# Projecting q, k and the third gate branch with seven products instead of eight in a two-layer encoder kernel

## The chip, the core and the metric

The kernel runs on one core of a Trainium2 chip. The metric is the device time of one execution in microseconds. Before the change it is 1118.29 us, the median of three runs (1117.27 to 1118.49). One execution was recorded with the hardware profiler; it took 1117.58 us, and its span from first to last instruction is 1115.3 us.

The engines are named as the profile names them: PE does matmuls (PEld is its weight load), DVE and ACT work elementwise, POOL does very little here, SP issues the DMAs. Each works through its own queue in order.

## The reference, cut to what matters

Two layers, each with a SwiGLU feed-forward block (FFN), a token-mixing block (mix) and a second FFN, on 256 tokens of width 1024 in float32. The change touches the mix:

```python
h = rms_norm(x, mix_pre_g[l])
u_pool, q_da, k_da, v_da, q_ca = jnp.split(h @ w_in[l], IN_SPLITS, axis=-1)
...
q = apply_partial_rope(q_da..., cos, sin)
k = apply_partial_rope(k_da..., cos, sin)
...
g_pool, g_da, g_ca = jnp.split(jax.nn.sigmoid(h @ w_gate[l] + b_gate[l]), N_BRANCH, axis=-1)
merged = (g_pool * (y_pool @ w_br_pool[l])
          + g_da * (y_da @ w_br_da[l])
          + g_ca * (y_ca @ w_br_ca[l]))
x = x + rms_norm(merged @ w_out[l], mix_post_g[l])
```

q and k together are 1024 columns of `w_in`, and so is `g_ca`, the third gate branch. Each is a product of 256x1024 tokens and a 1024x1024 weight.

## The kernel before

**Numbers in two parts.** PE multiplies fp32r, so every float32 operand is split into a high part (rounded by ACT) and a low part (the rest, by DVE), and one product is three matmuls, high x high, high x low and low x high (`mm3`, line 229, matmul at line 235). Weights come from memory in units of 128 partitions x 2048 columns (1 MB). `load_unit` (line 100) puts a unit into one of five `raw` buffers, and `split_unit` (line 113) makes its two parts in one of five pairs of tiles `wh` and `wl`: ACT casts (line 119), DVE subtracts (line 120), in two halves of 1024 columns, or in four quarters for the first five units of a stage (`fine`).

**The mix.** It has the normed, transposed tokens in an `xhl` tile (two chunks `c` of 128 tokens, eight blocks of 128 of the width). `pre_norm` (line 187) makes them while the FFN before is in its last matmuls: DVE gains and scales a chunk (lines 194 and 199), PE transposes it (line 207), ACT and DVE split it (lines 164 and 165). The mix then projects q and k (four units, 96 matmuls of 512 columns), turns them by RoPE (lines 627 to 630), transposes them for the scores (line 634), projects v (two units, 48 matmuls), then the pooling input and the cross-attention query (`form_a`, 96 matmuls of 256 columns), the memory keys and values (48), and the three gate branches (twelve units, 288). The attention's small matmuls are set between these: `place` and `issue_after` tie them to a matmul of that long row, counted in `fill`, at the positions in the `T_` tables at the top. Then `merged` (line 813) multiplies the three branches by their weights and by the gates, and `tail` (line 284) does the output projection and the norms of the next stage.

**Groups of seven in the FFNs.** The second FFN of both layers and the first of layer 1 already do some of their up-projections with Strassen's algorithm (in Winograd's form, `group`, line 384). The tokens are cut in two along the tokens and in two along the width (four blocks), the weight in four units `w11`, `w12`, `w21`, `w22`. Seven products of 12 matmuls then do the work of eight. For that, four sums of token blocks are made and split once (`token_sums`, line 374: four DVE operations of 512 columns, four ACT casts, four DVE subtracts), four sums of weight units (DVE, 128x2048, `add`, line 366), and seven sums of results (DVE, 128x512, the same line). `PLAN` sets such a group (`g`) among plain up (`u`) and down (`d`) projections. `pre_norm` keeps float32 copies of the token blocks for it (`keep`, line 212).

**Order.** The program is written in the order above; a scheduler of the framework then lays out each engine's queue by dependences and its own estimates, and buffers are taken in turn from pools of fixed depth. Weight loads go through SP's queue in the order of use.

## Time and profile before

| view | what it says |
|---|---|
| profiled execution | 1117.58 us, span 1115.3 us |
| three runs | median 1118.29 us, 1117.27 to 1118.49 |
| busy, share of the span | PEld 82%, ACT 58%, POOL 2% (PE and DVE in the prediction) |
| granted TensorE clock | 0.999 |
| weight loads | 189 of 1 MB, 4.8 us from issue to landing (median) |

How to read it: a matmul's own duration in the profile (393 ns) is longer than the distance to the next one, since matmuls are pipelined; the pieces of the chain of work show the distance. The chain of work that ended last is followed back from the last instruction, and names at each step the engine that was waited for. A row of the timeline merges instructions that follow one another: start in us, length in us, engine, line, operation, out<-in, count, and in brackets the idle time before it and what ended it.

### The profile page before, as it was taken

The page shows a single profiled execution, that of the slowest core. Times are in us where ns is not written, and L with a number is a line of the kernel's source. Part 1 is how long each engine was busy: PE and PEld are TensorE (multiplying, and loading weights), DVE is VectorE, ACT ScalarE, POOL GpSimd, SP SyncE. Part 2 cuts the span into 40 slices and gives each one's busy share as a digit, 9 for nine tenths or more (in the row PEclk, how much of TensorE's full clock was granted, in tenths as well). Part 3 has the DMA queues.
Part 4 walks back from the last instruction along what each step waited for, and adds up shares of the span by engine and source line. Part 5 has one row for each costly group of instructions (what it writes and reads, how often), then busy time and mean ns, then how long its engine had stood idle before and what let it go on. Part 6 is the DMA issues. An engine that isn't in the chain of part 4 may idle for free.

```text
span 1115.3 us, 13906 instructions
## 1 busy us (share of the span) xinstructions
PE 1106.0 (99%) x5247; PEld 912.4 (82%) x5247; DVE 892.5 (80%) x1215; ACT 652.0 (58%) x1082; POOL 25.0 (2%) x37
## 2 busy tenths in 40 slices
PE   9999999999999999999999999999999999999997
PEld 6888888888888888888888888888888888888886
DVE  6765556757857899999989999996676678999994
ACT  7656345646575557474675574765566647575571
POOL 0000000000000100000000000010000001000000
PEclk9999999999999999999999999999999999999999
DMA  9966543564563453563951736575445644273731
GB/s 343 385 239 227 214 150 130 189 227 144 198 218 139 173 205 132 209 244 135 332 199 71 302 118 221 201 269 196 170 172 191 236 158 175 89 254 138 286 114 38
DMA packets 35489, 218.27 MB, mean 196 GB/s; under 512 B 4192, under 2 KB 4448, under 8 KB 11232
## 3 DMA queue, kind: packets, MB, share of 16 engines
q1 hardware_dynamic: 35424, 217.40, 53.6%
q8 instruction: 41, 0.67, 0.2%
q14 instruction: 24, 0.20, 0.0%
HBM read 216.33 MB, written 1.05 MB: 195 GB/s over the span
## 4 chain that ended last, share of the span: by engine, by line
PE 97%; DMA 1%; ACT 1%; DVE 0%; POOL 0%; issue 0%; SPq 0%; DVEq 0%; POOLq 0%; ACTq 0%
PE ma L235 52%; PE acc L277 26%; PE mb L235 9%; PE acc L235 5%; PE mb L325 2%; PE mb L207 1%; PE acc L672 1%; PE acc L695 1%; PE mb L564 1%; DMA hid<-in_xt 1%; PE acc L758 1%; DMA raw<-in_w 0%; PE acc L742 0%; PE mb L831 0%; PE mb L634 0%; ACT wh L119 0%
## 5 line engine op out<-in xcount | busy, mean ns | idle before, releaser
L120 DVE TENSOR_TENSOR wl<-raw,wh 128x1024 fp32r<-128x1024 f32 (+1 forms) x498 | 524.5, 1093 | 99.2 <-ACT wh L119 96.8
L119 ACT CAST wh<-raw 128x1024 fp32r<-128x1024 f32 (+1 forms) x498 | 445.0, 949 | 198.0 <-DVE raw L366 62.1
L235 PE MATMUL ma<-wh,xhl 128*128 128x512 f32 x1664 | 529.8, 393 | 0.7 <-ACT wh L119 0.7
L235 PEld LDWEIGHTS ma<-wh,xhl 128*128 128x128 f32 x1664 | 311.5, 188 | 66.3 <-ACT wh L119 1.8
L235 PE MATMUL ma<-wl,xhl 128*128 128x512 f32 x832 | 327.0, 393 | 0.2 <-DVE wl L120 0.2
L277 PE MATMUL acc<-wh,hid 128*128 128x512 f32 x704 | 228.1, 395 | 0.0
L235 PEld LDWEIGHTS ma<-wl,xhl 128*128 128x128 f32 x832 | 156.4, 188 | 32.7 <-issue 1.0
L277 PEld LDWEIGHTS acc<-wh,hid 128*128 128x128 f32 x704 | 132.2, 188 | 27.0
L277 PE MATMUL acc<-wl,hid 128*128 128x512 f32 x352 | 136.7, 390 | 0.0
L235 PE MATMUL mb<-wh,xhl 128*128 128x512 f32 x280 | 90.4, 389 | 0.0
L366 DVE TENSOR_TENSOR raw<-raw 128x2048 f32<-128x2048 f32 x36 | 82.4, 2288 | 0.4
L277 PEld LDWEIGHTS acc<-wl,hid 128*128 128x128 f32 x352 | 66.3, 188 | 12.6
L235 PEld LDWEIGHTS mb<-wh,xhl 128*128 128x128 f32 x280 | 52.6, 188 | 10.9
L235 PE MATMUL mb<-wl,xhl 128*128 128x512 f32 x140 | 54.5, 389 | 0.0
L235 PE MATMUL acc<-wh,xhl 128*128 128x512 f32 x160 | 51.6, 391 | 0.0
L340 ACT ACTIVATE s<-ma 128x256 f32<-128x256 f32 x24 | 8.9, 386 | 64.6 <-PE ma L235 64.3
L148 POOL TENSOR_TENSOR sm<-sm,mhalf 128x1 f32<-128x1 f32 (+1 forms) x26 | 22.0, 846 | 1002.0 <-DVE sm L157 822.8
L155 ACT ACTIVATE junk<-acc 128x512 bf16<-128x512 f32 x24 | 14.4, 599 | 48.0 <-PE acc L277 48.0
L277 PE MATMUL acc<-wh,xhl 128*128 128x512 f32 x128 | 40.7, 394 | 0.0
L164 ACT CAST hid<-mb 128x256 fp32r<-128x256 f32 x88 | 32.1, 370 | 13.1 <-PE mb L325 10.3
L165 DVE TENSOR_TENSOR hid<-mb,hid 128x256 fp32r<-128x256 f32 x88 | 36.6, 419 | 1.6 <-ACT hid L164 1.4
L235 PEld LDWEIGHTS acc<-wh,xhl 128*128 128x128 f32 x160 | 30.0, 188 | 6.1
(161 smaller groups left out, 882.7 us busy)
## 6 DMA issues: line engine op xcount, KB each, us to landing
raw<-in_w SPq DMA_DIRECT2D x189, 1024.0 KB, 4.8
gain<-in_gains SPq DMA_DIRECT2D x17, 512.0 KB, 4.2
raw<-in_w SPq DMA_DIRECT2D x8, 256.0 KB, 5.6
hid<-in_memt SPq DMA_DIRECT2D x8, 256.0 KB, 7.5
hid<-in_xt SPq DMA_DIRECT2D x4, 256.0 KB, 5.3
raw<-in_w SPq DMA_DIRECT2D x2, 512.0 KB, 7.3
x<-in_x SPq DMA_DIRECT2D x4, 256.0 KB, 6.6
hid<-in_mem SPq DMA_DIRECT2D x4, 256.0 KB, 7.5
```

What stands on the lines that cost most here:

```text
L119: high = nc.scalar.copy(out=h[:, cs], in_=raw[:, cs])
L120: low = nc.vector.tensor_tensor(out=l[:, cs], in0=raw[:, cs], in1=h.bitcast(F32)[:, cs], op=ALU.subtract)
L148: nc.gpsimd.tensor_tensor(out=r, in0=v, in1=mhalf[:, :n], op=ALU.pow)
L155: sq.append(nc.scalar.activation(out=junk, in_=h, func=AF.Square, scale=fold / 32.0, accum_out=s[:, i:i + 1]))
L164: high = nc.scalar.copy(out=h, in_=ps)
L165: return high, nc.vector.tensor_tensor(out=l, in0=ps, in1=h.bitcast(F32), op=ALU.subtract)
L207: tps.append(nc.tensor.transpose(out=ps[:, k * P:(k + 1) * P], in_=xn[:, i * P:(i + 1) * P], identity=ident))
L235: done.append(nc.tensor.matmul(out=out, lhsT=lhsT, rhs=rhs, start=(first and i == 0), stop=(last and i == n - 1)))
L277: done.append(nc.tensor.matmul(out=banks[b], lhsT=a, rhs=ww[:, k, fs], start=(kk == first and k == 0 and i == 0), stop=(kk == last and k = ...
L325: nc.tensor.transpose(out=tp[:, u * P:(u + 1) * P], in_=hn[:, u * P:(u + 1) * P], identity=ident)
L366: nc.vector.tensor_tensor(out=out, in0=a, in1=b, op=ALU.add)
L564: ins.append(nc.tensor.transpose(out=tp[:, i * P:(i + 1) * P], in_=a[:, hh, kt * P:(kt + 1) * P], identity=ident))
```

## The change

q and k become one Strassen group at the start of the mix, with the first chunk of v in front of it and the second chunk of v in its middle. The first two gate branches stay as they are; the third becomes a second group at the end of the gates. Both use the same four token sums, which `token_sums` now makes once in the mix and which stay in one pair of `wh` and `wl` tiles until the second group is done. So of the five `wl` tiles, three are left for weights after the first group: `kv` (v and other results) keeps one as before, the sums another; of the five `wh` tiles `qkT` keeps one as before and the sums another. `pre_norm` now keeps the float32 token blocks for the mix too. The two `xhl` buffers become two named tiles, `xa` and `xb`, chosen by `slot`. The tokens of the memory (`mem_gain`) are no longer asked for in the FFN before, but in the mix, behind q and k. The results of the second half of q, k come out with a minus sign, which the copy of kT turns around (`sign`), as the bias addition does for the gates. The signs apart, what is computed is the same.

Core of the diff (`tokens_of`, `product`, `add`, `sums_tile` and `token_sums` are the FFN's helpers, moved out and made general; `...` marks what is left out):

```diff
-T_ROPE = 13
+T_ROPE = (13, 40)
...
-T_KT = (200, 222)
+T_KT = (152, 174)
...
-    xts = ctx.enter_context(tc.tile_pool(name="xts", bufs=2))
+    xts = ctx.enter_context(tc.tile_pool(name="xts", bufs=1))
...
+    def product(out, at, w):
+        wv = [t.rearrange("p (k m) -> p k m", k=4) for t in w]
+        return mm3(out, [(at(k), (wv[0][:, k, :], wv[1][:, k, :])) for k in range(4)])
+
+    def tokens_of(xx, c, b):
+        return lambda k: (xx[0][:, c, 4 * b + k, :], xx[1][:, c, 4 * b + k, :])
+
+    def add(out, a, b):
+        nc.vector.tensor_tensor(out=out, in0=a, in1=b, op=ALU.add)
+
+    def sums_tile(slot):
+        if slot is None:
+            sums = [wts.tile([P, 4 * 4, P], F32R, name=n) for n in ("wh", "wl")]
+        else:
+            t = xts.tile([P, 2, 4 * 4, P], F32R, name=("xa", "xb")[slot])
+            sums = [t[:, 0], t[:, 1]]
+        return sums, lambda j: (lambda k: (sums[0][:, 4 * j + k, :], sums[1][:, 4 * j + k, :]))
+
+    def token_sums(kept, sums):
+        a11, a12, a21, a22 = (kept[c, b] for c in range(2) for b in range(2))
+        s1 = t2()
+        nc.vector.tensor_tensor(out=s1, in0=a22, in1=a21, op=ALU.subtract)
+        nc.vector.tensor_tensor(out=a21, in0=a11, in1=a21, op=ALU.subtract)
+        nc.vector.scalar_tensor_tensor(out=a11, in0=s1, scalar=-1.0, in1=a11, op0=ALU.mult, op1=ALU.subtract)
+        nc.vector.scalar_tensor_tensor(out=a12, in0=a11, scalar=-1.0, in1=a12, op0=ALU.mult, op1=ALU.subtract)
+        for j, t in enumerate((s1, a11, a21, a12)):
+            split(t.rearrange("p (k t) -> p k t", t=P), sums[0][:, 4 * j:4 * j + 4, :], sums[1][:, 4 * j:4 * j + 4, :])
...
+        sums, summed = sums_tile(None)
+
+        def v_half(c):
+            ps = ma_bank()
+            now = form_b2(ps, ws[0], ws[1], c, xx)
+            nc.scalar.copy(out=v[:, c, :], in_=ps)
+            return now
+
+        qk = [s4.tile([P, D], F32, name="s4") for _ in range(2)]
+        s, u2, u3, v1 = (qk[c][:, b * 512:(b + 1) * 512] for c in range(2) for b in range(2))
+        ws = [next_unit() for _ in range(2)]
+        done = v_half(0)
+        w11, w12, w22, w21 = (next_raw() for _ in range(4))
+        pa, pe = ma_bank(), ma_bank()
+        done += product(pa, tokens_of(xx, 0, 0), split_unit(w11, 2))
+        nc.scalar.copy(out=u2, in_=pa)
+        done += product(pe, tokens_of(xx, 0, 1), split_unit(w21, 2))
+        add(s, u2, pe)
+        issue_after(late, done[T_UP])
+        token_sums(kept, sums)
+        v_half(1)
+        add(w11, w11, w12)
+        pd = mb_bank()
+        product(pd, summed(0), split_unit(w11, 2))
+        add(w11, w11, w22)
+        add(w12, w12, w22)
+        pb = mb_bank()
+        product(pb, summed(1), split_unit(w11, 2))
+        add(u2, u2, pb)
+        add(w21, w21, w11)
+        pc = ma_bank()
+        product(pc, summed(2), split_unit(w12, 2))
+        add(u3, u2, pc)
+        add(u2, u2, pd)
+        add(v1, u3, pd)
+        pf = mb_bank()
+        product(pf, summed(3), split_unit(w22, 2))
+        add(u2, u2, pf)
+        pg = ma_bank()
+        product(pg, tokens_of(xx, 1, 1), split_unit(w21, 2))
+
+        qkT = wts.tile([P, 2, 2, HEADS, P], F32, name="wh")
...
-        ws = [next_unit() for _ in range(4)]
-        done, wait = [], []
+        placed, fill = [], []
+        w = next_unit()
+
+        def place(at):
+            placed.append((at, []))
+            return placed[-1][1]
+
...
         for c in range(2):
-            qk = s4.tile([P, D], F32, name="s4")
-            for p in range(2):
-                ps = ma_bank()
-                now = form_b2(ps, ws[2 * p], ws[2 * p + 1], c, xx)
-                done += now
-                if c == 0 and p == 1:
-                    issue_after(late, done[T_UP])
-                issue_after(wait, now[T_ROPE])
-                wait = []
-                nc.scalar.copy(out=qk[:, p * 512:(p + 1) * 512], in_=ps)
-            g = qk.rearrange("p (g d) -> p g d", d=64)
+            if c == 1:
+                add(u3, u3, pg)
+            g = qk[c].rearrange("p (g d) -> p g d", d=64)
...
-            for dst, off in ((qT, 0), (kT, 512)):
+            wait = place(T_ROPE[c])
+            for dst, off, sign in ((qT, 0, 1.0), (kT, 512, -1.0)):
                 tp = mb_bank()
...
-                nc.scalar.copy(out=dst[:, c], in_=tp.rearrange("p (h t) -> p h t", h=HEADS))
-
-        mm = mm()
-        ws = [next_unit() for _ in range(2)]
-        fill, placed = [], []
-
-        def place(at):
-            placed.append((at, []))
-            return placed[-1][1]
-
-        for c in range(2):
-            ps = ma_bank()
-            now = form_b2(ps, ws[0], ws[1], c, xx)
-            fill += now
-            issue_after(wait, now[T_ROPE])
-            wait = []
-            nc.scalar.copy(out=v[:, c, :], in_=ps)
-
-        w = next_unit()
+                    wait.append(nc.tensor.transpose(out=tp[:, h * P:(h + 1) * P], in_=qk[c][:, off + h * P:off + (h + 1) * P], identity=ident))
+                nc.scalar.activation(out=dst[:, c], in_=tp.rearrange("p (h t) -> p h t", h=HEADS), func=AF.Copy, scale=sign)
+        mm = mem_gain(l, 1 - slot)
+
...
-        for br in range(3):
+        for br in range(2):
...
+        bias = gain(l * 10 + 9)
+        s, u2, u3, v1 = (hids.tile([P, 512], F32, name="hid") for _ in range(4))
+        w11, w12, w22, w21 = (next_raw() for _ in range(4))
+
+        def gate_product(at, w):
+            ps = ma_bank()
+            fill.extend(product(ps, at, split_unit(w, 2)))
+            return ps
+
+        nc.scalar.copy(out=s, in_=gate_product(tokens_of(xx, 0, 0), w11))
+        add(w11, w11, w12)
+        nc.scalar.copy(out=v1, in_=gate_product(summed(0), w11))
+        add(w11, w11, w22)
+        add(w12, w12, w22)
+        add(u2, s, gate_product(summed(1), w11))
+        add(u3, u2, gate_product(summed(2), w12))
+        add(u2, u2, v1)
+        add(v1, u3, v1)
+        add(s, s, gate_product(tokens_of(xx, 0, 1), w21))
+        add(w21, w21, w11)
+        add(u2, u2, gate_product(summed(3), w22))
+        add(u3, u3, gate_product(tokens_of(xx, 1, 1), w21))
+        for (b, c), t, sign in (((0, 0), s, 1.0), ((1, 0), u2, -1.0), ((0, 1), u3, 1.0), ((1, 1), v1, -1.0)):
+            nc.vector.scalar_tensor_tensor(out=t, in0=t, scalar=sign, in1=bias[:, b * 512:(b + 1) * 512], op0=ALU.mult, op1=ALU.add)
+            gates[2, b, c] = t
...
-                nx["xx"] = xt_pair()
-                nx["kept"] = {} if stages[i + 1][0] == "ffn" else None
+                nx["slot"] = slot if kind == "ffn" else 1 - slot
+                nx["xx"] = xt_pair(nx["slot"])
...
         wi = a["w_in"][l]
-        for s in (256, 768, 1280):
-            wide(wi, slice(s, s + 512))
+        wide(wi, slice(1280, 1792))
+        for half, col in ((0, 256), (0, 768), (1, 768), (1, 256)):
+            block(wi, half, col)
         for s in (0, 1792):
             cols(wi, slice(s, s + 256))
         wide(a["w_mem_kv"][l], slice(0, 512))
-        for i in range(6):
+        for i in range(4):
             wide(a["w_gate"][l], slice(512 * i, 512 * i + 512))
+        for half, col in ((0, 2048), (0, 2560), (1, 2560), (1, 2048)):
+            block(a["w_gate"][l], half, col)
         br = np.concatenate([a["w_br_pool"][l], a["w_br_da"][l], a["w_br_ca"][l]], axis=0)
         for i in range(2):
```

**What moves on DVE at the start of the mix.** The names: line 157 to 199 (the same in both) is the norm of chunk 1, line 165 on `xhl` or `xa` the split of its transposed tokens, line 120 a weight's low part, line 176 the memory tokens, 627 to 630 RoPE. DVE's queue of before, from the norm of chunk 1:

```order
L157 TENSOR_SCALAR sm<-sm 128x1
L194 TENSOR_TENSOR s_1652<-x_89,gain 128x512 x2
L199 TENSOR_SCALAR s_1652<-s_1652,sm 128x512 x2
L120 TENSOR_TENSOR wl<-raw,wh 128x512 x2
L176 SCALAR_TENSOR_TENSOR xhl<-hid,colt,xhl 128x2x128 x5
L165 TENSOR_TENSOR xhl<-mb,xhl 128x512 x2
L176 SCALAR_TENSOR_TENSOR xhl<-hid,colt,xhl 128x2x128 x3
L627 TENSOR_TENSOR s_1791<-s_1738,csd 128x256
L628 TENSOR_TENSOR s_1792<-s_1738,snd 128x16x8
L629 TENSOR_TENSOR s_1792<-s_1738,snd 128x16x8
L630 TENSOR_TENSOR s_1738<-s_1791,s_1792 128x16x16
```

And of the change, where line 275 is `add` and lines 288 to 291 are the sums in `token_sums`:

```order
L199 TENSOR_SCALAR s4_1647<-s4_1647,sm_1657 128x512 x2
L120 TENSOR_TENSOR wl_1751<-raw_1740,wh_1750 128x1024
L165 TENSOR_TENSOR xa_1561<-mb_1661,xa_1561 128x512
L165 TENSOR_TENSOR xa_1561<-mb_1670,xa_1561 128x512
L120 TENSOR_TENSOR wl_1751<-raw_1740,wh_1750 128x1024
L120 TENSOR_TENSOR wl_1770<-raw_1746,wh_1769 128x1024 x2
L288 TENSOR_TENSOR s2_1788<-s2_1677,s2_1668 128x512
L275 TENSOR_TENSOR raw_1740<-raw_1740,raw_1742 128x2048
L275 TENSOR_TENSOR s4_1688<-s4_1688,ma_1749 128x512
L289 TENSOR_TENSOR s2_1668<-s2_1585,s2_1668 128x512
L165 TENSOR_TENSOR wl_1687<-s2_1788,wh_1686 128x512
L290 SCALAR_TENSOR_TENSOR s2_1585<-s2_1788,s2_1585 128x512
```

(`wl_1751` is the low part of `w11`, `wl_1770` that of `w21`, `wl_1687` holds the token sums, `raw_1740` is `w11` itself.) Before, chunk 1's norm was followed by the rest of k's last unit, the memory tokens and RoPE; now it is followed by the low parts of `w11` and `w21`, and then by a row of sums. In layer 0 the memory tokens have gone ahead of the norms, into the last part of the FFN. Behind the rows shown, DVE goes on with the three other token sums and their splits, three weight sums in a row, and the low parts of the other five products, with six sums of results among them.

**What moves on PE there.** Names with their buffer numbers: `mb_1666` and `mb_1673`, now `mb_1661` and `mb_1670`, take the transposes of chunk 1's tokens. Before, from the end of k's first unit:

```order
L235 MATMUL ma_1765<-wl_1717,xhl_1570 128x512
L235 MATMUL ma_1765<-wh_1716,xhl_1570 128x512
L235 MATMUL ma_1765<-wh_1728,xhl_1570 128x512
L207 MATMUL mb_1666<-ident_92,s4_1652 128x128 x4
L207 MATMUL mb_1673<-ident_92,s4_1652 128x128 x4
L235 MATMUL ma_1765<-wl_1729,xhl_1570 128x512
L235 MATMUL ma_1765<-wh_1728,xhl_1570 128x512 x2
```

And of the change, from the end of v's first chunk (`ma_1714`), where `ma_1748` is the product with `w11` and `ma_1749` that with `w21`:

```order
L235 MATMUL ma_1714<-wl_1705,xa_1561 128x512
L235 MATMUL ma_1714<-wh_1704,xa_1561 128x512
L235 MATMUL ma_1748<-wh_1750,xa_1561 128x512
L235 MATMUL ma_1749<-wh_1769,xa_1561 128x512
L207 MATMUL mb_1661<-ident_92,s4_1647 128x128 x4
L207 MATMUL mb_1670<-ident_92,s4_1647 128x128 x4
L235 MATMUL ma_1748<-wl_1751,xa_1561 128x512
L235 MATMUL ma_1748<-wh_1750,xa_1561 128x512 x2
```

Before, 36 matmuls and one more of the mix stood ahead of the transposes. Now it is 26: the 24 of v's first chunk and one each of the products with `w11` and `w21`, those that need only a high part; the two products' other matmuls follow the transposes.

**What moves on DVE at the end of the gates.** Lines 796 (before) and 823 (change) add a gate's bias to a finished bank, line 535 and 543 look for a softmax's maximum, 747 and 774 are its reciprocal, 752 its scaling, 705 to 715 and 732 to 742 the attention's norm. Before, around the last score matmuls:

```order
L705 TENSOR_SCALAR sm_2346<-sm_2337 128x4
L708 TENSOR_TENSOR s2_2350<-acc_2286,sm_2348 128x512
L120 TENSOR_TENSOR wl_2764<-raw_2761,wh_2763 128x1024 x2
L715 SCALAR_TENSOR_TENSOR xhl_2239<-mb_2352,gsub_104,xhl_2239 128x512
L120 TENSOR_TENSOR wl_2772<-raw_2769,wh_2771 128x1024
L796 TENSOR_TENSOR hid_2687<-ma_2662,gain_2617 128x512
L535 TENSOR_REDUCE sm_2372<-acc_2359 128x2
L535 TENSOR_REDUCE sm_2372<-acc_2360 128x2
L120 TENSOR_TENSOR wl_2772<-raw_2769,wh_2771 128x1024
L537 TENSOR_SCALAR sm_2375<-sm_2372 128x4
L120 TENSOR_TENSOR wl_2834<-raw_2831,wh_2833 128x1024 x2
L747 RECIPROCAL sm_2383<-sm_2371 128x4
```

And of the change, where `raw_2805` is the second group's `w11`, `raw_2807` its `w12`, `raw_2809` its `w22`, and `ma_2772` the last plain gate:

```order
L275 TENSOR_TENSOR raw_2805<-raw_2805,raw_2807 128x2048
L275 TENSOR_TENSOR raw_2807<-raw_2807,raw_2809 128x2048
L732 TENSOR_SCALAR sm_2386<-sm_2377 128x4
L823 TENSOR_TENSOR hid_2770<-ma_2745,gain_2657 128x512
L735 TENSOR_TENSOR s2_2390<-acc_2326,sm_2388 128x512
L120 TENSOR_TENSOR wl_2836<-raw_2805,wh_2835 128x1024 x2
L742 SCALAR_TENSOR_TENSOR xb_2279<-mb_2392,gsub_104,xb_2279 128x512
L823 TENSOR_TENSOR hid_2797<-ma_2772,gain_2657 128x512
L275 TENSOR_TENSOR raw_2805<-raw_2805,raw_2809 128x2048
L543 TENSOR_REDUCE sm_2412<-acc_2399 128x2
L543 TENSOR_REDUCE sm_2412<-acc_2400 128x2
L120 TENSOR_TENSOR wl_2858<-raw_2805,wh_2857 128x1024
```

Three of the four weight sums of the second group stand here among the softmax, each 2048 columns wide, and the low parts in between belong to its products. Before, there were only low parts.

More of the change, by code (lines that the diff above doesn't have):

```diff
@@ L168, in halves, with xt_pair @@
         return [t[:, 0:512], t[:, 512:1024]]
-    def xt_pair():
-        t = xts.tile([P, 2, 2, KT, P], F32R, name="xhl")
+    def xt_pair(slot):
+        t = xts.tile([P, 2, 2, KT, P], F32R, name=("xa", "xb")[slot])
         return t[:, 0], t[:, 1], t.rearrange("p s c k t -> p (s c) k t")
@@ L295, in tail, with ffn @@
         return tps
-    def ffn(i, xx, late, kept, g_post, finish, ahead, raw_rstd=None):
+    def ffn(slot, xx, late, kept, g_post, finish, ahead, raw_rstd=None):
         fine[0] = FINE
@@ L355, in up_both @@
                 if kept and p == 2 and c == 0:
[L356 to L360 removed]
+                    token_sums(kept, sums)
         def tokens(c, b):
[L363 to L366 removed]
+            return tokens_of(xx, c, b)
         if kept:
[L369 to L382 removed]
+            sums, summed = sums_tile(1 - slot)
         def group(p):
@@ L584, in mem_gain, with mix @@
             loaded.append(t)
-        def scaled():
-            for b, t in enumerate(loaded):
-                for i in range(2):
-                    k = 2 * b + i
-                    col = 3 * DEPTH + KT + KT * l + k
-                    gained_split((mm[0][:, :, k, :], mm[1][:, :, k, :]), t[:, i], colt[:, col:col + 1])
-            return mm
-        return scaled
-    def mix(l, xx, late, mm, finish):
+        for b, t in enumerate(loaded):
+            for i in range(2):
+                k = 2 * b + i
+                col = 3 * DEPTH + KT + KT * l + k
+                gained_split((mm[0][:, :, k, :], mm[1][:, :, k, :]), t[:, i], colt[:, col:col + 1])
+        return mm
+    def mix(l, slot, xx, late, kept, finish):
         fine[0] = FINE
@@ L600, in mix @@
         colb = l * 3
-        qkT = wts.tile([P, 2, 2, HEADS, P], F32, name="wh")
-        qT, kT = qkT[:, 0], qkT[:, 1]
         kv = wts.tile([P, 2048], F32, name="wl")
@@ L606, in mix @@
         kc = kv[:, 1536:2048].rearrange("p (t s) -> p t s", t=2)
+        sums, summed = sums_tile(None)
[15 more added lines that the diff above has]
+        issue_after(late, done[T_UP])
+        token_sums(kept, sums)
+        v_half(1)
[19 more added lines that the diff above has]
+        qkT = wts.tile([P, 2, 2, HEADS, P], F32, name="wh")
+        qT, kT = qkT[:, 0], qkT[:, 1]
         held = rawp.tile([P, 2048], F32, name="raw")
@@ L806, in mix @@
         preload(AF.Silu, sg)
-        mg = xt_pair()
+        mg = xt_pair(slot)
         turns = []
@@ L882, in finish @@
             if c == 0:
-                nx["xx"] = xt_pair()
-                nx["kept"] = {} if stages[i + 1][0] == "ffn" else None
+                nx["slot"] = slot if kind == "ffn" else 1 - slot
+                nx["xx"] = xt_pair(nx["slot"])
+                nx["kept"] = {}
                 nx["g"] = gain(stages[i + 1][1] * 10 + stages[i + 1][2])
@@ L892, in ahead @@
                     mem_scale()
-                if row == 0:
-                    nx["mem"] = mem_gain(l)
-            late = ffn(i, cur, late, kept, gain(l * 10 + row + 1), finish, ahead, [rst[:, c:c + 1] for c in range(2)] if i == 0 else None)
-        else:
-            late = mix(l, cur, late, mem, finish)
-        cur, mem, kept = nx.get("xx"), nx.get("mem"), nx.get("kept")
+            late = ffn(slot, cur, late, kept, gain(l * 10 + row + 1), finish, ahead, [rst[:, c:c + 1] for c in range(2)] if i == 0 else None)
+        else:
+            late = mix(l, slot, cur, late, kept, finish)
+        slot, cur, kept = nx.get("slot"), nx.get("xx"), nx.get("kept")
 def _constants(np):
```

29 lines of the change are left out of this document (5 added, 24 removed).

## The prediction

> **What bounds the kernel now.** I read the page first, then the chain of waits, then stretches and single rows. The page's rows of busy time and of the chain:
>
> ```profile
> span 1115.3 us, 13906 instructions
> PE 1106.0 (99%) x5247; PEld 912.4 (82%) x5247; DVE 892.5 (80%) x1215; ACT 652.0 (58%) x1082; POOL 25.0 (2%) x37
> ...
> PE 97%; DMA 1%; ACT 1%; DVE 0%; POOL 0%; issue 0%; SPq 0%; DVEq 0%; POOLq 0%; ACTq 0%
> ```
>
> 97% of the chain is PE, so a matmul taken out is worth its distance to the next one, as long as nothing else comes last. The distance stands in the chain, in order of time, in a stretch of 48 matmuls; the rows below it are the start of the mix of layer 0 (the transposes of chunk 0, the first matmuls, the transposes of chunk 1) and, for later, the first product of a group of the FFN:
>
> ```profile
> 31.12 10.94 PE ma L235 x48
> ...
> 191.77 0.87 PE mb L207 x8
> 192.65 2.09 PE acc L277 x9
> 194.74 8.39 PE ma L235 x37
> 203.13 0.87 PE mb L207 x8
> ...
> 427.65 5.44 PE mb L235 x24
> ```
>
> 10.94 / 48 = 0.228 us a matmul. The pieces join: PE does not wait from 191.77 to 204.00. An average hides how near DVE is, so the next view is busy time in stretches: two in the FFN of layer 0 that already has groups of seven, then the mix's start, and from the memory's keys to the last gate.
>
> ```profile
> core 0: us, PE busy (x) PEld busy (x) DVE busy (x) ACT busy (x) POOL busy (x), PEclk, DMA share, GB/s
> 407.00:425.00 18.00, 18.00 (x87) 14.91 (x86) 17.44 (x22) 7.23 (x15) 0.00 (x0) 1.00 0.14 57
> 425.00:457.00 32.00, 32.00 (x146) 26.47 (x145) 30.96 (x34) 23.98 (x30) 0.00 (x0) 1.00 0.60 223
> ...
> 194.60:229.90 35.30, 35.30 (x170) 29.49 (x168) 25.75 (x46) 22.61 (x41) 2.08 (x2) 1.00 0.58 208
> ...
> 243.50:339.50 96.00, 95.74 (x487) 78.20 (x488) 65.95 (x112) 59.79 (x126) 2.06 (x2) 1.00 0.50 178
> ```
>
> Where a group stands, DVE is 97% busy, with PE still fed. In the mix's start it is 73% busy (25.75 of 35.30), in the gates 69%. That is the room there is.
>
> **The change, part by part.** *Matmuls.* Two groups of seven per layer instead of eight products each: 12 fewer matmuls a group, 48 in all, 48 x 0.228 = 10.9 us, 5.5 a layer. This is certain, the program has 48 fewer at line 235.
>
> *What a group costs DVE.* The rows by form, and a pair of rows of the timeline where such instructions stream:
>
> ```profile
> L120 DVE TENSOR_TENSOR wl<-raw,wh 128x1024 fp32r<-128x1024 f32 x378 | 448.7, 1221 | 88.9 <-ACT wh L119 86.7 <-issue 1.3 <-PE ma L235 0.4
> L366 DVE TENSOR_TENSOR raw<-raw 128x2048 f32<-128x2048 f32 x36 | 82.4, 2288 | 0.4
> L366 DVE TENSOR_TENSOR s<-s,mb 128x512 f32<-128x512 f32 x36 | 24.7, 687 | 0.9 <-PE mb L235 0.9
> ...
> 220.15 4.63 DVE L120 TENSOR_TENSOR wl<-raw,wh 128x1024 fp32r<-128x1024 f32 x4
> ...
> 408.50 4.61 DVE L366 TENSOR_TENSOR raw<-raw 128x2048 f32<-128x2048 f32 x2
> ...
> 417.50 0.69 DVE L165 TENSOR_TENSOR xhl<-s,xhl 128x512 fp32r<-128x512 f32 x1
> 418.10 0.69 DVE L379 SCALAR_TENSOR_TENSOR s<-s,s 128x512 f32<-128x512 f32 x1
> ```
>
> In a stream an instruction starts a little before its predecessor ends: a low half takes 1.16 us (4.63 / 4), a weight sum 2.26, an operation of 512 columns 0.60 (418.10 - 417.50). A group is 14 low halves, 4 weight sums and 7 sums of results: 16.2 + 9.0 + 4.2 = 29.4 us of DVE, against 84 x 0.228 = 19.1 us of PE. So a group starves PE unless DVE enters it some 10 us ahead.
>
> *The group of q and k.* In the changed order DVE does nothing for the group until chunk 1's norm is over. That norm waits on ACT, so its rows of before set the clock:
>
> ```profile
> 191.12 1.67 ACT L119 CAST wh<-raw 128x512 fp32r<-128x512 f32 x3 [0.61 <-PE acc L277]
> 192.70 1.06 ACT L164 CAST xhl<-mb 128x512 fp32r<-128x512 f32 x2
> ...
> 195.22 0.60 ACT L155 ACTIVATE junk<-acc 128x512 bf16<-128x512 f32 x1
> ...
> 213.69 3.93 ACT L119 CAST wh<-raw 128x1024 fp32r<-128x1024 f32 x4
> ...
> 199.35 0.21 DVE L157 TENSOR_SCALAR sm<-sm 128x1 f32<-128x1 f32 x1
> ...
> 201.21 0.88 DVE L199 TENSOR_SCALAR s<-s,sm 128x512 f32<-128x512 f32 x2 [0.44 <-POOL sm L148]
> ```
>
> From 191.12, when a `wh` tile comes free, ACT now has two half casts of w11 (0.98 each, 3.93 / 4), the pair at line 164 (1.06), a half cast of w21 and the two kept copies of chunk 0 (line 212, of the pair's size, 1.06): 196.1, where the square at line 155 stood at 195.22. So the chain behind it is 0.9 us later, and L199 ends at 203.0 instead of 202.1. From there the queue holds, in order and without a gap that I can find: 14 low halves, 4 weight sums, 4 token sums and their 4 splits, 2 splits of chunk 1 and 6 sums of results, 16.2 + 9.0 + 16 x 0.60 = 34.8 us. It is over at 237.8; the last product's second half then needs 5 more matmuls: 238.9. PE has 24 + 12 x 7 + 24 = 132 matmuls there and 0.87 of transposes, from 194.74: without a wait it would be done at 225.7. So PE waits **13.2 us**. The waits can be named: some 2 us at chunk 1's transposes, which now stand behind 26 matmuls instead of 37; about 2 for the low part of w11; 1 for w11+w12; then the largest, near 7 us with two matmuls in it, while DVE does three weight sums in a row (6.7 us) before the first low part that uses one. No later stage gives this back, since PE was not waiting before. Bounds: 12.3 if L199 keeps its old end; 15.7 with the mean durations of the rows (1221, 2288, 687 ns: 37.3 us). I take 13.2, the streamed one.
>
> *The group of the gates.* Here DVE has slack before, and two of the four weight sums stand ahead of the last plain gate. From the end of that gate's products (I call it G) DVE has 18 low halves (14 less 4 done, and the 8 of merged's four units), 2 weight sums, 8 operations of 512 columns, 4 bias additions, and the softmax, 4 maxima and 8 scalings, and 4 splits:
>
> ```profile
> L804 ACT ACT_TABLE_LOAD x2 | 2.6, 1283 | 0.0
> ...
> 298.71 1.28 DVE L535 TENSOR_REDUCE sm<-acc 128x2 f32<-128x512 f32 x2
> ...
> 304.04 1.14 DVE L752 TENSOR_SCALAR s<-s,sm 128x256 f32<-128x256 f32 x4
> ...
> 297.38 1.93 PE acc L742 x16
> 299.31 8.43 PE ma L235 x36
> 307.74 0.87 PE mb L564 x8
> ...
> 312.93 1.51 PE acc L758 x16
> ...
> 317.37 0.86 PE mb L779 x4
> ```
>
> 18 x 1.16 + 2 x 2.26 + 8 x 0.60 + 4 x 0.60 + 4 x 0.62 + 2 x 1.14 + 4 x 0.45 + 0.5 of small ones = 39.7 us. PE has to the same point 84 + 48 matmuls, 30.1 us, and 1.93 + 2 x 0.87 + 2 x 1.51 + 0.86 = 7.5 of attention: 37.6. DVE starts its list between 0.6 and 2.2 us after G, waits for ACT between 0 and 3.3 us (an estimate: ACT's own row of casts and exponentials ends about 1.6 us behind DVE's need at two places), and PE has six matmuls (1.4) behind the last low part. So PE waits between 0.6 + 39.7 + 1.4 - 37.6 = 4.1 and 2.2 + 39.7 + 3.3 + 1.4 - 37.6 = 9.0 us. ACT has twelve sigmoids in the same stretch, and three buffers are left where four were; I take 6.5, near the middle, as I could not see which of ACT's waits falls together with DVE's.
>
> *The memory tokens.* Their loads now stand behind the pool weight, which waits for a raw buffer that v's second unit frees at 180.8:
>
> ```profile
> 179.50 1.29 DVE L120 TENSOR_TENSOR wl<-raw,wh 128x512 fp32r<-128x512 f32 x2
> ...
> 185.44 0.60 ACT L155 ACTIVATE junk<-acc 128x512 bf16<-128x512 f32 x1 [3.40 <-PE acc L277]
> ...
> hid<-in_memt SPq DMA_DIRECT2D x8, 256.0 KB, 7.5
> raw<-in_poolw SPq DMA_DIRECT2D x2, 128.0 KB, 2.9
> ```
>
> In layer 0 ACT has five of their casts, and DVE five subtractions, ahead of chunk 0's squares at 185.44. With 2.9 us to land nothing is late, with 7.5 they land at 188.3 and chunk 0's transposes, which PE reaches without a wait at 191.77, are 2.9 us late. I take 1 us; layer 1 has them behind that norm, at nothing.
>
> *At nothing:* the kept copies of chunk 1 (ACT is 64% busy there, 22.61 of 35.30, and would cost 1.06 us if it were not); two more table loads a layer, since a sigmoid now stands behind the preload (1283 ns each, 2.6 us if the merge waited for ACT, which I hold inside the 9.0); the sign in the copies; RoPE, the same instructions behind the group, with the pooling's 48 matmuls to hide them; and the bytes, which stay the same.
>
> **Sum.** A layer: -5.5 + 13.2 + 6.5 = +14.2. Two layers and the 1 us: +29.4. Against the profiled execution, 1117.6, that is 1147.0; the median of the three runs is 0.7 higher: **1148**. The bounds give 1117.6 + 2 x (-5.5 + 12.3 + 4.1) = 1139 and 1117.6 + 2 x (-5.5 + 15.7 + 9.0) + 2.9 = 1159.
>
> **The rivals.** *DVE is ahead, and the matmuls count.* The price: 1118.3 - 10.9 = 1107. The place is the stretch before each group, and it decides at 10.7 us: so much of q and k's list would have to be done before L199 ends. For it: in the FFN just that happens, two weight sums begun at 408.50 are over at 413.1, and the group's products that start at 427.65 find them done 14.5 us ahead. Against it: in the mix no instruction of the list stands ahead of that norm in DVE's queue. Change by nothing, a lead of about half, is the same mechanism.
>
> *Only the first group starves.* If ACT and DVE get through the gates in time: 1118.3 + 2 x (-5.5 + 13.2) = 1134. For it: DVE is 69% busy in the gates before. Against it: the 39.7 us above against 37.6.
>
> *PE loses its rate in the waits.* The first matmuls of the program run slower than all later ones:
>
> ```profile
> 1.19 4.88 PE L869 MATMUL acc<-s 128*128 128x512 bf16 x11 [1.19 <-DVE s L866]
> ```
>
> That is 0.444 us each. If the 7 us wait brought that rate back for the four products behind it, 48 x 0.444 = 21.3 us from 226.8 would end at 248.1 instead of 238.9: 9.2 us a layer, 1166. The Trainium skill ("TensorE: Matmul & The Clock Gate", Part 1: The HAM clock gate) has a rule of this kind: PE's clock is halved after an idle window of about 3.4 us and returns after a busy one. By it the slow stretch would be short; eight matmuls of 0.444 instead of 0.228 are an estimate of 1.7 us a wait, and DVE, which sets the end of the group, would hide most of it. Nothing before the first matmuls in this trace shows such a wait, so it neither agrees nor differs. That the change does not do what it says is no rival: the 48 matmuls are gone from the program.
>
> **How the numbers follow.** Forecast (both groups starve) 0.64, only the first 0.13, the slow clock 0.08, matmuls count 0.10, within 0.2% 0.05. Faster 0.10, same 0.05, slower 0.85; 0.2%, 2.2 us, is about what a measurement of this kernel tells from no change. The range reaches from below the one-group case, 1128, to the clock's, 1168, and leaves out the 0.15 of the first and the last. The forecast's own range is 1139 to 1159.
>
> **What would show it.** The chain of waits should name DVE at lines 120 and 275 with some 13 us in q and k's stretch of each layer, and 4 to 9 in the third gate; DVE should be near 100% busy from L199 to the last low part, some 35 us; the longest gap of PE should stand before the product with w11+w22, right behind three DVE sums of 128x2048. Chunk 1's transposes should be waited for by about 2 us. It is wrong if PE stays above 97% busy through the mix's first 45 us, or if the group's weight sums stand in gaps of DVE before the norm ends.

## The result, and the profile after

| | before | change |
|---|---|---|
| median of 4 runs, us | 1117.78 | 1149.42 |
| span of the profiled run, us | 1115.3 | 1147.8 |

The ratio is 1.0284 (95% interval 1.0267 to 1.0300): 31.6 us slower, where 29.4 were forecast. From the page of the changed kernel, the rows that answer to those of before:

```profile
span 1147.8 us, 13958 instructions
...
PE 1110.5 (97%) x5199; PEld 906.3 (79%) x5199; DVE 979.2 (85%) x1299; ACT 686.3 (60%) x1124; POOL 24.9 (2%) x37
...
PE 84%; DVE 7%; ACT 4%; DMA 2%; issue 2%; POOL 1%; SPq 0%; DVEq 0%; POOLq 0%; ACTq 0%
```

PE was 97% of the chain and is 84%: 13% has passed to engines that PE waits for, DVE first. To see where, the mix is divided at three instructions that both kernels have: the transposes of chunk 0, the first score matmuls, and the first transposes of the next block. In layer 0 they stand in PE's timeline before the change as

```profile
191.61 1.03 PE L207 MATMUL mb<-ident,s 128*128 128x128 f32 x8
...
241.50 1.78 PE L672 MATMUL acc<-wh 64*128 64x256 f32 x14
...
378.65 1.04 PE L207 MATMUL mb<-ident,s 128*128 128x128 f32 x8
```

and in the changed kernel as

```profile
193.93 1.07 PE L207 MATMUL mb<-ident,s 128*128 128x128 f32 x8 [1.39 <-DVE s L199]
...
254.09 2.00 PE L699 MATMUL acc<-wh 64*128 64x256 f32 x16
...
394.88 1.04 PE L207 MATMUL mb<-ident,s 128*128 128x128 f32 x8
```

The first stretch (q, k, v and the pooling) took 49.89 us and takes 60.16, the second (gates, attention, merge, output projection) 137.15 and 140.79; 2.3 us are lost ahead of both. In layer 1 the stretches are 49.93 and 137.17 before, 61.76 and 141.63 after. 2.3 + 10.3 + 3.6 + 11.8 + 4.5 = 32.5, the difference of the spans. Each stretch also has 12 matmuls of line 235 (2.74 us) less, so PE loses 13.0 and 14.6 us in the first beside what it saves, 6.4 and 7.2 in the second. Not all of that is waiting: in the first stretch PE is idle for 8.9 and 9.3 us, where before it was not, and the rest are longer matmuls (the granted clock is 0.94 and 0.92 there, before 1.00). In the second it is idle for 4.9 and 4.5.

The 2.3 us ahead of layer 0's stretch are the memory tokens: ACT waits for their load, and the squares of chunk 0's norm (line 155) stand behind them, at 187.17 instead of 185.44:

```profile
185.96 1.31 ACT L175 ACTIVATE xb<-hid,colt 128x256 fp32r<-128x256 f32 x3 [2.03 <-DMA hid<-in_memt]
```

PE's waits in the first stretch of layer 0 (in brackets the idle time and what ended it; the last row but one is one of some ten matmuls that follow one another at a distance of 0.43 us):

```profile
207.08 0.50 PE L235 MATMUL ma<-wl,xa 128*128 128x512 f32 x1 [0.69 <-DVE wl L120]
...
219.54 0.50 PE L235 MATMUL mb<-wl,wh 128*128 128x512 f32 x1 [1.47 <-DVE wl L120]
...
225.07 0.80 PE L235 MATMUL mb<-wh 128*128 128x512 f32 x1 [4.11 <-ACT wh L119]
226.97 0.80 PE L235 MATMUL ma<-wh 128*128 128x512 f32 x1 [1.10 <-ACT wh L119]
...
228.42 0.63 PE L235 MATMUL mb<-wh 128*128 128x512 f32 x1
...
239.73 0.50 PE L235 MATMUL ma<-wl,xa 128*128 128x512 f32 x1 [0.68 <-DVE wl L120]
```

The 4.11 us are put down to ACT. ACT's row says whom it waited for, and DVE's row why:

```profile
223.97 7.68 ACT L119 CAST wh<-raw 128x1024 fp32r<-128x1024 f32 x8 [6.35 <-DVE raw L275]
```

```profile
202.68 0.88 DVE L199 TENSOR_SCALAR s<-s,sm 128x512 f32<-128x512 f32 x2
203.48 1.22 DVE L120 TENSOR_TENSOR wl<-raw,wh 128x1024 fp32r<-128x1024 f32 x1
...
219.40 6.81 DVE L275 TENSOR_TENSOR raw<-raw 128x2048 f32<-128x2048 f32 x3
226.13 4.62 DVE L120 TENSOR_TENSOR wl<-raw,wh 128x1024 fp32r<-128x1024 f32 x4
```

The cast needs the second of three weight sums in a row. From the end of the norm to 1.1 us past the group's last low part DVE is busy 35.76 of 37.30 us (engines in the order PE, PEld, DVE, ACT, POOL, then PE's clock):

```profile
203.50:240.80 37.30, 28.88 (x116) 22.03 (x115) 35.76 (x38) 17.47 (x24) 0.00 (x0) 0.91 0.29 101
```

In the second stretch most of the waiting is at the merge, past the group (all rows but the first):

```profile
329.76 0.50 PE L235 MATMUL ma<-wh 128*128 128x512 f32 x1 [0.80 <-ACT hid L834]
...
349.61 0.50 PE L235 MATMUL ma<-wh,xb 128*128 128x512 f32 x1 [0.88 <-ACT wh L119]
...
353.18 0.50 PE L235 MATMUL ma<-wl,xb 128*128 128x512 f32 x1 [1.69 <-DVE wl L120]
...
358.40 0.72 PE L235 MATMUL ma<-wh,xb 128*128 128x512 f32 x2 [0.44 <-ACT wh L119]
```

### The profile page after: what moved, and what is told of

The parts are those of the page before. It is cut to its first block, busy times and chain, and to the rows that moved or that the text cites. A ratio compares the mean times of both kernels' runs of the same rounds, so it can differ in the third digit from the quotient of the medians.

```text
span 1147.8 us, 13958 instructions
## 1 busy us (share of the span) xinstructions
PE 1110.5 (97%) x5199; PEld 906.3 (79%) x5199; DVE 979.2 (85%) x1299; ACT 686.3 (60%) x1124; POOL 24.9 (2%) x37
## 4 chain that ended last, share of the span: by engine, by line
PE 84%; DVE 7%; ACT 4%; DMA 2%; issue 2%; POOL 1%; SPq 0%; DVEq 0%; POOLq 0%; ACTq 0%
PE ma L235 42%; PE acc L305 24%; PE mb L235 9%; PE acc L235 4%; DVE wl L120 2%; DVE raw L275 2%; ACT wh L119 2%; PE mb L353 2%; DMA raw<-in_w 1%; PE acc L699 1%; PE mb L207 1%; POOL sm L148 1%; ACT junk L155 1%; DMA hid<-in_xt 1%; PE acc L785 1%
## 5 line engine op out<-in xcount | busy, mean ns | idle before, releaser
L235 PE MATMUL ma<-wh,xa 128*128 128x512 f32 x824 | 264.7, 393 | 1.5 <-ACT wh L119 1.1
L235 PE MATMUL ma<-wh,xb 128*128 128x512 f32 x680 | 219.8, 393 | 2.2 <-ACT wh L119 1.3
L235 PEld LDWEIGHTS ma<-wh,xa 128*128 128x128 f32 x824 | 154.4, 188 | 35.4 <-ACT wh L119 2.6
L235 PE MATMUL ma<-wl,xa 128*128 128x512 f32 x412 | 161.9, 393 | 3.8 <-DVE wl L120 3.8
L235 PEld LDWEIGHTS ma<-wh,xb 128*128 128x128 f32 x680 | 127.3, 188 | 29.5 <-ACT wh L119 2.1
L235 PE MATMUL ma<-wl,xb 128*128 128x512 f32 x340 | 133.6, 393 | 3.3 <-DVE wl L120 3.3
L275 DVE TENSOR_TENSOR raw<-raw 128x2048 f32<-128x2048 f32 x52 | 118.8, 2287 | 0.6
L235 PEld LDWEIGHTS ma<-wl,xa 128*128 128x128 f32 x412 | 77.4, 188 | 21.9 <-DVE wl L120 6.4
L235 PEld LDWEIGHTS ma<-wl,xb 128*128 128x128 f32 x340 | 63.9, 188 | 17.4 <-DVE wl L120 4.6
L235 PE MATMUL mb<-wh,xa 128*128 128x512 f32 x176 | 57.9, 396 | 0.0
L368 ACT ACTIVATE s<-ma 128x256 f32<-128x256 f32 x24 | 8.9, 385 | 61.3 <-PE ma L235 60.9
```

The lines of the kernel that those rows point to most:

```text
L235: done.append(nc.tensor.matmul(out=out, lhsT=lhsT, rhs=rhs, start=(first and i == 0), stop=(last and i == n - 1)))
L275: nc.vector.tensor_tensor(out=out, in0=a, in1=b, op=ALU.add)
```

## The experiments

Medians, and the two stretches of layer 0 and 1 divided as above (the ratios are to the runs of the kernel before on the same chip, whose medians lay between 1117.45 and 1117.93):

| run | median, us | ratio to before (95%) | first stretch | second stretch |
|---|---|---|---|---|
| before | 1117.8 | | 49.9, 49.9 | 137.2, 137.2 |
| change | 1149.4 | 1.0284 (1.0267 to 1.0300) | 60.2, 61.8 | 140.8, 141.6 |
| qk_only | 1142.8 | 1.0222 (1.0206 to 1.0237) | 60.4, 61.8 | 137.5, 137.6 |
| gate_only | 1131.6 | 1.0132 (1.0115 to 1.0149) | 51.7, 52.3 | 140.8, 140.9 |
| no_sums | 1126.6 | 1.0074 (1.0057 to 1.0091) | 49.9, 51.1 | 139.9, 140.8 |
| pool_sums | 1190.5 | 1.0651 (1.0636 to 1.0667) | 68.8, 70.7 | 152.0, 152.5 |
| late_preload | 1147.6 | 1.0265 (1.0251 to 1.0279) | 60.6, 60.9 | 140.0, 139.9 |
| no_sums_late | 1118.3 | 1.0007 (0.9999 to 1.0016) | 49.9, 51.2 | 135.8, 135.8 |
| memt_late | 1150.0 | 1.0286 (1.0272 to 1.0300) | 61.7, 62.0 | 140.8, 140.8 |
| warm | 1149.0 | 1.0281 (1.0267 to 1.0295) | 59.1, 61.5 | 140.8, 140.8 |
| gate_dve | 1117.9 | 1.0001 (0.9992 to 1.0010) | 49.9, 49.9 | 138.0, 138.0 |
| gate_dma | 1145.8 | 1.0255 (1.0238 to 1.0272) | 49.9, 49.9 | 151.2, 152.1 |
| both_dma | 1190.5 | 1.0649 (1.0631 to 1.0668) | 63.4, 69.2 | 154.5, 154.5 |
| shift | 1142.3 | 1.0220 (1.0206 to 1.0234) | 60.2, 61.7 | 138.0, 138.0 |

**Each group alone.** qk_only has the third gate as in the kernel before:

```diff
-        for br in range(2):
+        for br in range(3):
...
-        bias = gain(l * 10 + 9)
-        s, u2, u3, v1 = (hids.tile([P, 512], F32, name="hid") for _ in range(4))
...
```

> Only the group of q and k; the third gate stands as two plain products each, as before the change. Theory (each group is held up by DVE's own list in its own stretch): the q and k stretch is as in the change (first scores 12.6 us later than before in layer 0, of it 2.2 at the memory tokens, and 11.8 more in layer 1), and from the scores to the merge nothing is lost or won: 1117.8 + 12.6 + 11.8 = 1142 us. Rival (the loss in the gates comes from the new order, the held pair or the sigmoids, not from the group itself): the gate stretch stays 6 to 7 us a layer longer, 1155 us, since the 12 matmuls that paid for a part of it are back.

1142.8: the theory's 1142. The first stretch is the change's, the second that of before within 0.4 us. gate_only instead has q and k as plain products:

```diff
-        w11, w12, w22, w21 = (next_raw() for _ in range(4))
-        pa, pe = ma_bank(), ma_bank()
...
+        wqk = [[next_unit(), next_unit()]]
+        done += qk_half(0, 0)
...
```

> Only the group of the third gate; q and k are plain products in the order of the change, the token sums are made and the pair is held as in the change. Theory (own list): q and k cost nothing but the 2.2 us of the memory tokens in layer 0, the gates 3.6 and 4.5 us as in the change: 1117.8 + 2.2 + 8.1 = 1128 us. Rival (DVE comes late into the gates because the first group has put it behind): the gate group pays its 12 matmuls, 1117.8 + 2.2 - 5.5 = 1114.5 us.

The second stretch agrees (3.6 and 3.7 us, the rival has -2.7); the total is 3.4 us over the theory, since the first stretch is 1.8 and 2.3 us longer than before. PE waits 1.80 and 2.19 us for a low part there; that the held pair leaves too few buffers for v, q and k at once is possible, and was not tried by itself. Each group's cost stays when the other is gone.

**The weight sums.** no_sums leaves all 16 out and shows what they cost; its results are not those of the reference.

```diff
-        add(w11, w11, w12)
...
-        add(w11, w11, w22)
-        add(w12, w12, w22)
...
-        add(w21, w21, w11)
```

> The 16 weight sums of the mix's groups are left out (the products then use the plain weights). Theory (DVE's list): 9.0 us less a group; q and k keep 3 to 6 us of waits a layer, the gates none: 1149.4 - 2 x (8.5 + 6.5) = 1119 us, between 1114 and 1126. Rival (ACT's casts, the late weight loads or the three buffers set the pace): less than 4 us a layer are won, 1141 us or more.

In q and k the theory holds: 9.0 us of DVE gone, 10.3 and 10.7 us won, and the stretch is within 1.2 us of that of before, with 12 matmuls fewer in it. The surplus goes with the slow clock (below), which is 1.00 again here. (With the sums the casts also lose what they wait for, and this run can't tell the two apart; that DVE's list is the limit rests also on its 35.76 busy us of 37.30, and on its length, below.) In the gates the theory does not hold: only 0.9 us a layer are won where 6.5 were expected. PE waits at the merge as before, now for ACT:

```profile
340.04 0.50 PE L235 MATMUL ma<-wh,xb 128*128 128x512 f32 x1 [2.15 <-ACT wh L119]
341.30 0.79 PE L235 MATMUL ma<-wl,xb 128*128 128x512 f32 x1 [0.76 <-DVE wl L120]
```

and ACT's row ahead of it holds no cast of weights from 326.0 to 339.0, but sigmoids, copies and three loads of a table, the last two around the preload:

```profile
335.61 1.28 ACT L535 ACT_TABLE_LOAD   x1
336.90 0.20 ACT L535 ACTIVATE sm<-mhalf 128x1 f32<-128x1 f32 x1
337.13 1.28 ACT L848 ACT_TABLE_LOAD   x1
338.42 0.63 ACT L848 ACTIVATE hid<-hid 128x512 f32<-128x512 f32 x1
```

The other way round, the sums stay and DVE is relieved by POOL:

```diff
+    def wadd(out, a, b):
+        nc.gpsimd.tensor_tensor(out=out, in0=a, in1=b, op=ALU.add)
...
-        add(w11, w11, w12)
+        wadd(w11, w11, w12)
...
```

> The 16 weight sums of the mix's groups run on POOL instead of DVE. Theory (DVE's list sets the end): 9.0 us a group leave DVE; POOL is idle there, and if its sum takes about twice DVE's 2.26 us and the two engines do not disturb each other, the last sum of q and k ends about when it does now, and some 3 to 9 us a layer are won in q and k and 4 to 6 in the gates: 1120 to 1136 us. Rival (POOL's reading of SBUF shuts DVE's two-operand instructions out): each sum then costs DVE more than its own 2.26 us, and the time rises to 1150 to 1185 us.

1190.5, above even the rival's range. From DVE's timeline while POOL's first two sums run (207.21 to 218.11), and POOL's group:

```profile
213.62 5.04 DVE L291 TENSOR_TENSOR s<-s,s 128x512 f32<-128x512 f32 x1
218.69 0.69 DVE L292 TENSOR_TENSOR s<-s,s 128x512 f32<-128x512 f32 x1
```

```profile
L278 POOL TENSOR_TENSOR raw<-raw 128x2048 f32<-128x2048 f32 x16 | 76.4, 4773 | 97.7 <-DVE wl L120 52.8 <-ACT s L577 44.4
```

A subtraction of 0.69 us took 5.04 and ended 0.6 us after POOL's second sum: DVE stood still for 4.35 us. A sum costs POOL 4.77 us instead of DVE's 2.29, and DVE pays most of that too: in layer 0's first stretch it is busy for 57.0 us, where the change has 53.7 with four sums of 2.29 in it, so each sum on POOL lengthens DVE's other work by about 3.1 us.

**The gates: ACT's table.**

```diff
-        preload(AF.Silu, sg)
+                    sgs.append(sg)
+        last = preload(AF.Silu, None)
+        for sg in sgs:
+            issue_after([last], sg)
```

> The change, with the loading of the Silu table put behind all twelve sigmoids of a layer, so that ACT loads two tables fewer a layer (2 x 1.28 us) and casts the merge's weights earlier. Theory A (ACT's own row holds up the merge: sigmoids and tables ahead of the casts): the waits at the merge (0.9 + 1.7 + 0.3 + 0.4 us) shrink by 1.5 to 2.6 a layer, 1149.4 - 2 x 2 = 1145 us, with the q and k stretch unchanged. Theory B (DVE's list holds up the gates, as forecast): the merge waits for DVE as before, 1149 us.

> As no_sums (the 16 weight sums of the mix's groups left out), and the Silu table behind all sigmoids. Theory A (with the sums gone, ACT's row alone holds up the merge): the waits of 2.2 + 0.8 us there and the slow clock behind them go, 1126.6 - 2 x 3.5 = 1119.5 us, down to 1116. If neither ACT nor DVE is the limit there but the weight loads or the three buffers: 1125 us or more.

Alone, the later table wins 0.8 and 1.7 us a layer in the second stretch, between A and B. Of the merge's waits, two stay: 0.9 us for casts that stand behind four sigmoids in ACT's row, and 1.7 for DVE; the two smaller ones (0.3 and 0.4) are gone. Without the sums it wins 4.1 and 5.0 us, and the group keeps 1.4 of its 2.74. So two rows hold up the merge side by side: taking away DVE's sums wins 0.9, ACT's tables 1.3, both 5.4 (means of the layers).

**The gates: where the attention stands.** gate_dve is the kernel before with the gate group alone, its pair made once v is out of the buffers, and the later table:

```diff
+        sums, summed = sums_tile(None)
+        token_sums3(kept, sums)
 
         def da_scores(c, ins):
...
```

> The kernel before, with the third gate alone as a group (sums on DVE as in the change, the Silu table behind all sigmoids, token sums made once q, k and v are out of the weight buffers, the memory tokens where they were). Theory (the gate group is held up by DVE's list and ACT's row, whatever stands before it): nothing is lost in q and k, and the gates lose what late_preload shows, 2.7 us a layer: 1117.8 + 5.4 = 1123 us. Rival (late buffers and the stage's new order are a part of it): the group pays, 1113 to 1116 us.

1117.9, neither of the two: the second stretch is 0.8 us longer, not 2.7, and the whole is level with the kernel before. Even of the 0.8 most is where the stretch ends: the next block's transposes stand here three matmuls further down in PE's row (18 matmuls of the output projection follow them, 21 in the kernel before and in the change), which is 0.7 us. So the group costs 0.1 to 0.2 us a layer. From its first scores to its last ones PE needs 55.8 us, in the change 67.4: the tables that set the attention's matmuls among the others count in a list that lost v's 48 matmuls, and of them only `T_KT` was taken down by 48. (`token_sums3` is gate_dve's copy of `token_sums`.) The run shift takes the rest down too, with everything else as in late_preload:

```diff
-T_SC = (242, 336)
+T_SC = (194, 288)
-T_DA = (186, 210, 278, 302)
+T_DA = (138, 162, 230, 254)
...
-T_CA = (372, 396)
+T_CA = (324, 348)
...
```

> As late_preload, with the numbers that place the attention's matmuls among the gates' all taken down by 48 (the change took v's 48 matmuls out of the list they count in, and moved only two of them). The attention then stands as far behind its first scores as before the change, and 48 matmuls (10.9 us) of plain gate come between the last scores and the group's end, as in gate_dve. Theory C (the gate group waits because the attention's softmax, copies and sigmoids fall into the group's own stretch, where they share DVE and ACT with it): the stretch from the first scores to the next block's transposes falls from 139.95 us to about the 138.0 of gate_dve, 1147.6 - 2 x 2 = 1143.5 us. Rival (the group's list is the limit wherever the attention stands, and gate_dve's gain came from its weight buffers or order): 1147 to 1149 us.

1142.3, and the second stretch is 138.0 in both layers, that of gate_dve to 0.01 us, with the transposes as far down as there. That makes the gain over late_preload 2.0 and 0.7 us a layer, which are the 5.2 us between the medians. Its waits at the end of the gates:

```profile
346.26 0.50 PE L235 MATMUL ma<-wl,xa 128*128 128x512 f32 x1 [0.17 <-DVE wl L120]
...
350.40 0.50 PE L235 MATMUL ma<-wh,xb 128*128 128x512 f32 x1 [0.60 <-DVE hid L275]
351.54 0.50 PE L235 MATMUL ma<-wl,xb 128*128 128x512 f32 x1 [0.63 <-DVE wl L120]
```

Theory C holds. Beside the q and k group alone (1142.8), this is what the gate group is worth: about nothing. What is left, 24 us over gate_dve, is the group of q and k with the order of the stage that goes with it.

**The memory tokens.**

```diff
-                gained_split((mm[0][:, :, k, :], mm[1][:, :, k, :]), t[:, i], colt[:, col:col + 1])
+                issue_after(gained_split((mm[0][:, :, k, :], mm[1][:, :, k, :]), t[:, i], colt[:, col:col + 1]), behind)
...
-        mm = mem_gain(l, 1 - slot)
+        mm = mem_gain(l, 1 - slot, group_end)
```

> The change, with the memory tokens' 8 casts and 8 subtractions a layer behind q and k's group instead of before and in it. Theory (in layer 0 they hold chunk 0's norm up by 2.2 us, part of which q and k's waits would hide; in layer 1 some stand in DVE's list of the group, which makes its stretch 11.8 us longer than before where layer 0 has 10.4): layer 0's first transposes are back at 191.8, both q and k stretches lose what DVE is spared, 8 x 0.42 us at most: 1149.4 - 2 to 4 = 1146.5 us. Rival (q and k's list starts with the norm whatever stands before, so that the 2.2 us come back as a longer wait): 1149 us, or above it by what the 16 instructions now cost ahead of the first scores.

The rival, by the median. The profiled execution runs 0.9 us behind that of the change already ahead of the tokens (the last transposes of the FFN at 177.66 instead of 176.77), so times are taken from there. Layer 0's transposes of chunk 0 then stand where they did before the change, 14.8 us on (17.2 in the change): the 2.3 us are gone. Chunk 1's transposes are 1.6 us earlier than in the change, the group's last wait 1.9, and the scores, which now have the 16 instructions ahead of them, 0.8; so are the next block's transposes, and the medians don't show it (1150.0 and 1149.4). About two thirds of what the tokens cost PE ahead of q and k comes back behind when they are moved. (The table counts from the 14 score matmuls at 254.19; two more stand ahead of them.)

**The clock.**

```diff
+        spare = acc_bank()
+        filler = [nc.tensor.matmul(out=spare, lhsT=xx[0][:, 0, 0, :], rhs=xx[0][:, 0, 0:4, :], start=True, stop=True) for _ in range(17)]
+        in_order([before_gap[-1], *filler, after_gap[0]])
```

> The change, with 17 more matmuls of 128x512 into a bank that nobody reads, in the largest wait of q and k's group (4.1 us before the product with w11+w12+w22). They take 17 x 0.228 = 3.9 us of that wait. Theory (the granted clock falls to a half because PE was idle for about 4 us; DVE sets the end anyway): the clock stays 1.00, the ten matmuls of 0.43 us behind the wait take 0.23, and as DVE waits 1.3 us for PE there, 0.5 to 1.5 us a layer are won: 1147.5 us, between 1146 and 1149. Rival (the clock has nothing to do with the idle time, or power lowers it): the ten stay at 0.43 us, 1149.5 us. If the filler overruns the wait it costs: 1150 to 1152.

Behind its largest wait PE's matmuls are slow, and the filler keeps PE busy in that wait. The changed kernel in layer 0, with PE idle from 220.97 to 225.07, and then the one with the filler:

```profile
217.00:222.00 5.00, 2.49 (x10) 1.42 (x8) 4.79 (x5) 0.62 (x2) 0.00 (x0) 1.00 0.00 0
222.00:226.00 4.00, 0.80 (x1) 0.29 (x1) 3.97 (x2) 2.03 (x3) 0.00 (x0) 0.82 0.00 0
226.00:230.00 4.00, 3.04 (x7) 2.40 (x8) 4.00 (x5) 4.00 (x5) 0.00 (x0) 0.50 0.12 16
```

```profile
222.00:226.00 4.00, 3.43 (x14) 2.26 (x13) 3.96 (x2) 1.94 (x3) 0.00 (x0) 1.00 0.00 0
226.00:230.00 4.00, 2.94 (x12) 2.28 (x13) 4.00 (x5) 4.00 (x6) 0.00 (x0) 1.00 0.13 16
```

In layer 0 the clock (the number behind POOL's) stays at 1.00, the matmuls behind the wait take 0.23 us, and the stretch is 1.1 us shorter: DVE, which in the change waits 1.30 us for the product that runs at the low clock, waits 0.23. In layer 1 the clock fell all the same, for eight matmuls, and only 0.3 us are won there. The total, 0.5 us, is inside the scatter of the runs.

**Sums by transfers that add.**

```diff
+    def wadd(out, src):
+        nc.gpsimd.dma_start(out=out, in_=src, accum_op=ALU.add)
...
-        add(w11, w11, w12)
+        wadd(w11, w_d[n12])
...
```

> As gate_dve, with the four weight sums of the group done by transfers that add to the buffer (three from HBM, one from the buffer of the other sum), so that DVE is spared 9.0 us a layer. Theory (DVE's list is the limit that is left once the table is moved): as no_sums_late shows, 1.5 us a layer are won, up to the 2.7 of the matmuls: 1117.8 - 3 to 5.5 = 1113.5 us. Rival (a transfer that adds takes longer than the 4.9 us that a plain load of such a block takes from issue to landing, and two stand in a row): the products wait for the buffers, 1119 to 1135 us.

> The change with the Silu table behind all sigmoids and the 16 weight sums of both groups done by transfers that add. Theory (DVE's list sets the end of q and k): with transfers as quick as plain loads it comes near no_sums_late, 1118 to 1124 us. Rival (in q and k, which have no lead, two transfers in a row take longer than DVE's sums, 6.8 us for three): 1130 us or more.

Both times the rival, and gate_dma (1145.8) is beyond the rival's range. From gate_dma's view of the transfers (KB each, median us from issue to landing):

```profile
raw<-in_w SPq DMA_DIRECT2D x189, 1024.0 KB, 4.9
...
raw<-in_w POOLq DMA_DIRECT2D x6, 1024.0 KB, 8.5
...
raw<-raw POOLq DMA_DIRECT2D x2, 1024.0 KB, 8.1
```

Each sum lands 8 us after its issue (8.6 and 7.0 in both_dma), and DVE's takes 2.3. In layer 0's gates of gate_dma ACT waits 6.2, 4.3 and 6.0 us for such transfers ahead of its casts, and PE's longest waits, 6.7 and 3.2 us, are for ACT.

## Why the prediction was right, point by point

- **The matmuls:** 12 fewer in each stretch, 48 in all. That they are worth 10.9 us where nothing waits no run shows; the nearest, no_sums_late, keeps 1.4 of the 2.74 in the gates.
- **q and k, 13.2 us a layer:** 13.0 and 14.6 measured, and the theory of DVE's list holds, by no_sums and by the list's length. From the end of the norm to the last low part it takes 36.1 us in layer 0, where 34.8 were forecast; with the filler it takes 35.0. So the list itself was right, and a second price stood behind it that the sum held at nothing: the half clock, 1.1 us, since DVE waits for a product. The pieces were less exact than the sum. The wait at chunk 1's transposes (2 us) is nearly missing (0.45 us ahead of them), since the memory tokens had already set PE back by 2.3; the low part of w11 cost 1.1 in two waits, not 2; w11+w12 1.5, not 1; the largest gap 5.2 with one matmul in it, not 7 with two, and it ended behind the second of the three sums. That layer 1 has 1.6 us more is mostly the place of the dividing line: in layer 0 the tokens push the first transposes back, ahead of the stretch, and with the tokens out of the way (memt_late) the two are 61.7 and 62.0.
- **The gates, 6.5 us a layer:** 6.4 and 7.2. That it came so close is in part luck: 6.5 was the middle of 4.1 to 9.0, for want of a reading of ACT's waits. The list had the softmax, the bias additions and the splits of the attention in the same stretch as the group, and that is the largest part of the cause: with the later table the loss is 5.5 us, and with the attention 48 matmuls earlier too it is 2.9, about what the 12 matmuls save. What the prediction did not see is that the attention need not have been there. And the two table loads that it held inside its upper bound are a limit of their own beside DVE.
- **The memory tokens, 1 us:** 2.3 in layer 0, by the late load that the prediction named, none in layer 1; moved behind the group they win nothing in the median, so most of this term and part of q and k's are the same wait. By the spans the rise is 32.5 us where the sum had 29.4: 1.3 more here, 1.2 in q and k, 0.6 in the gates.
- **The rivals:** that the matmuls count would have needed DVE's list to be done ahead of the norm; no part of it was. (The 10.7 us at which the prediction lets this rival be decided don't follow from its sum, which asks for a lead of 13.2; nothing else rests on them.) That only the first group starves is refuted by gate_only. The slow clock was real, but for some ten matmuls and not for 48.
